# A hybrid attention, convolution and mixture-of-experts layer on one core: the second norm's scale and shift moved to the experts' transposed rows, f32 router logits, another PSUM bank for the last projection, first low parts later

## The chip, the cores and the metric

The kernel runs on one core of a Trainium2 chip. The metric is the device time of one execution in microseconds (us). The engines are called by their names in the profile: PE (TensorE matmul), DVE (VectorE), ACT (ScalarE), POOL (GpSimd) and SP (SyncE, which issues the weight loads).

## The reference, cut to what matters

All tensors are f32; there are 1024 tokens of width 1024, and 16 experts with hidden width 1024.

```python
h2 = modulate(rmsnorm(x, g_ffn), sh2, sc2)     # r*g_ffn*(1+sc2) + sh2, per column
aff = softmax(h2 @ w_router)                   # 1024 x 16
g, idx = top_k(aff.T, 128)                     # each expert takes its 128 best tokens
xs = h2[idx]                                   # per expert 128 x 1024
a, u = xs @ w_gate[e], xs @ w_up[e]
y = (silu(a) * u) @ w_down[e] * g
x = x + gt2 * scatter_add(y, idx)
out = rmsnorm(x, g_final)
```

Ahead of this stand the modulation vectors, the first norm, windowed attention woven with a short convolution, and the output projection `x + gt1 * (mix @ w_out)`.

## The kernel before, in words

**f32 from two parts.** The large products keep f32 accuracy by splitting each operand: a high part (a cast) and a low part (the operand minus its high part). Each product is then three matmuls: high by high, high by the weights' low part, the activations' low part by the weights' high part. A matrix of 1024 x 1024 is taken in eight row blocks k; each k takes six matmuls of 128x512, in this order: two high by high, two on the weights' low part, two on the activations' low part. One matrix so takes 48 matmuls. For each k ACT makes the weights' high part (tile `whl`, L1142) and DVE the low part (L1145), from raw f32 rows that SP loads (`split_rows`, `pump`).

**The projection stage.** `project(t)` (L862) projects one tile of 128 tokens, `residual` adds it to x, `rms` squares it on ACT and takes the reciprocal root on POOL (`rstd`), and `gained` (L885) multiplies x by a row S2 that holds g_ffn*(1+sc2). For the last tile (t = 7) the second half of the columns is done in two quarters c = 0, 1, whose PSUM banks are `po2` (L909): a bank of the P0 tag and the bank C1 (`p1(1)`). C1 is also where the sort keeps `pa`, the transposed affinities (L1047).

**Routing.** Beside the projection of tile t, PE, DVE and ACT route tile t-1 (`route`): `turn_x2` transposes x, splits it into high and low parts (`x2s`: ACT L955, DVE L956), `logits_T` multiplies them by the split router weights (`plT` L970, `lgT` L973, `pl` L977), and `finish_h2` (L930) makes h2 = (x*S2)*rstd + B2 on DVE and has SP store it. Tile 7 goes another way: f32 transposes, and `logits` on f32 operands (L964). Then follow the softmax (L992 is its first step), a sort of each expert's column (MAX8 and MATCH_REPLACE8, L1057 and L1059) and merges of sorted lists (L1020, L1021, L1077). The smallest kept affinity of each expert is `thr` (L1225).

**The step to the experts.** From `thr`: a mask, the places of the chosen tokens (`place`, `choose`: `pos`, `oh`, `pi`, `idx`), and `gather(e)`, an indirect DMA on POOL that fetches the 128 rows of h2 (tile `xr`). The first weights, the gate matrix of expert 0, are split ahead of this, in the tail of the projection stage (`pre_split` L1192).

**An expert.** `turn_x(e)` (L1310) calls `transpose_split`: eight transposes on PE into two PSUM tiles (`xTp`, four blocks of 128x128 each), two casts on ACT and two subtractions on DVE, all reading PSUM. `gate_part` is the 48 matmuls `pg`, `up_part` the 48 `pu`, `down_part` the 48 `py`; ACT takes the Silu of `pg` (tile `hid`), DVE multiplies it by `pu` (L1335), `turn_h` transposes and splits the result (`hTt`).

**What sets the order.** PE's order is the written one: `turn_x(e+2)` is called from the `up_part` of expert e+1 after three quarters of its matmuls, then come the last 12 `pu`, and then the `pg` of expert e+2, which are the first to use the transposed rows. ACT's and DVE's order in the expert stage is set by a list scheduler at build time; each engine then runs its instructions strictly in that order.

Of the kernel before, what the change touches and what calls it, by code (L numbers as in the profile page):

```python
# [9 lines left out]
F32 = mybir.dt.float32  # L10
# [75 lines left out]
def tile_layer(ctx, tc, x, c, cx, c_ctx, w_ada, b_ada, g_mix, w_in, conv_w, sink, w_out, g_ffn,  # L86
# [562 lines left out]
    def router_consts():  # L649
# [28 lines left out]
        rt.update(triu=triu, iota1=iota1, tokid=tokid, wr=wr, lbias=lbias)  # L678
# [148 lines left out]
    rowsb, s_rows1 = crow["a"], crow["sa"]  # L827
    rowsc, s_rows2 = slots.get((2, D), F32, "rowsB")
    GT1, S2, B2 = rowsb[:, 0], rowsb[:, 1], rowsc[:, 0]
    bcast_row(B2, rows_d[1])  # L830
    bcast_row(S2, rows_d[2])
    gf = wm("gf")
    bcast_row(gf, g_ffn[0])
    nc.vector.scalar_tensor_tensor(S2, S2, 1.0, gf, op0=OP.add, op1=OP.mult)

    triu, iota1, tokid, wr, lbias = [rt[k] for k in ('triu', 'iota1', 'tokid', 'wr', 'lbias')]

    wmem = work.tile([128, 384], F32R, tag="mp", name="wrs")
    wrs, ident2 = shaped(wmem, (KC, 2, NE)), wmem[:32, 256:272].bitcast(F32)
    nc.vector.tensor_copy(wrs[:, :, 0], wr)  # L840
    nc.vector.tensor_tensor(wrs[:, :, 1], wr, wrs[:, :, 0].bitcast(F32), op=OP.subtract)
    nc.vector.tensor_tensor(wmem[:32, 256:272], ident[:32, 0:16], ident[:32, 16:32], op=OP.add)

    fold, sign = wmem[:, 272:336].bitcast(F32), wmem[:, 336:337].bitcast(F32)
    nc.vector.tensor_tensor(wmem[:, 272:336], ident[:, 0:64], ident[:, 64:128], op=OP.add)
# [16 lines left out]
    def project(t):  # L862
# [22 lines left out]
        def gained(cols):  # L885

            nc.vector.tensor_tensor(h2_of[t][:, cols], xt[:, cols], S2[:, cols], op=OP.mult)

        if t < NT - 1:
# [7 lines left out]
            gained(slice(0, D))  # L897
        else:
# [9 lines left out]
            gained(slice(0, 512))  # L908
            po2 = [p2(0, "po")[:, 0], p1(1, "po")]  # L909
            for c in range(2):  # L910
                cols = slice(512 + 256 * c, 768 + 256 * c)
                for k in range(KC):
                    hi, lo = ah[:, 0, k], ah[:, 1, k]
                    for a, j, first, last in ((hi, 0, k == 0, False), (hi, 1, False, False), (lo, 0, False, k == KC - 1)):
                        mm(po2[c][:, 0:256], a, wo[k // 4, 1][j][:, k % 4, 256 * c:256 * c + 256],
                           start=first, stop=last, skip_group_check=True)
                        yield 0.108
                with tc.high_priority():
                    nc.vector.tensor_tensor(xt[:, cols], po2[c][:, 0:256], xt[:, cols], op=OP.add)
                    nc.scalar.activation(h2_of[t][:, cols], xt[:, cols], AF.Square, accum_out=ssq[:, 8 + c:9 + c])  # L920
                gained(cols)
# [8 lines left out]
    def finish_h2(t):  # L930
        h2 = h2_of.pop(t)
        x2_of.pop(t)
        nc.vector.scalar_tensor_tensor(h2, h2, rstd[:, t:t + 1], B2, op0=OP.mult, op1=OP.add)
        h2_done[t] = h2
        if t < NT - 2:
            store_h2(t)
# [6 lines left out]
    def turn_x2(t, g, ks=None):  # L943
        if t < NT - 1:
            x2T_of[t, g] = (wm, w4)[g]("x2s", (4, 2, 128), F32R)
        elif g == 0:
            x2T_of[t] = wm("x2T")
# [18 lines left out]
    def logits_T(t):  # L966

        pl = p1(0, "plT")
        for k in range(KC):
            mm(pl[:2 * NE, :256], wrs[:, k].rearrange("p a b -> p (a b)"),  # L970
               x2T_of[t, k // 4][:, k % 4].rearrange("p a b -> p (a b)"), start=k == 0, stop=k == KC - 1)
        lgT = work.tile([32, 256], F32, tag="up", name="lgT")
        nc.scalar.copy(lgT, pl[:32, :256])  # L973
        yield 0.8
        pl_of[t] = p1(0, "pl")
        for i in range(2):
            mm(pl_of[t][:, :NE], lgT[:, i * 128:(i + 1) * 128], ident2, start=i == 0, stop=i == 1)  # L977
# [220 lines left out]
    with order_of:  # L1198
# [5 lines left out]
        slots.put(*wo[0, 1][2:], *wo[1, 1][2:], s_rows1)  # L1204
# [7 lines left out]
        slots.put(s_rows2)  # L1212
# [5 lines left out]
        pre_split((2,))  # L1218
        split_rows("g", 0, 3, (0,))
# [91 lines left out]
    def turn_x(e):  # L1311
        st[e] = {"x": transpose_split(xrow.pop(e), "xT")}
# [195 lines left out]
```

## Time and profile before

| | |
|---|---|
| median of 3 runs | 1176.4 us (1175.99 to 1176.52) |
| the profiled execution | 1177.61 us, its span 1175.8 us |
| mean granted TensorE clock | 0.96 of full speed |
| PE busy | 1064.8 us (91%) |
| DVE busy | 982.2 us (84%) |
| ACT busy | 770.2 us (66%) |
| POOL busy | 357.1 us (30%) |

All times in rows are microseconds from the start of the span; the profiled execution took 1.8 us more than its span. The stages by time: to 440 everything ahead of the output projection, 440 to 545 the projection of tiles 0 to 7 with the routing of the tile before, 545 to 592 the last quarter matmuls, the rest of sorting and the step to the experts, 592 to 1127 the experts, then the end. A share of busy time alone does not tell what bounds a stage: that is read from the waits and the chain of work that ended last.

### The profile page before, as it was taken

The page shows a single profiled execution, that of the slowest core. Times are in us where ns is not written, and L with a number is a line of the kernel's source. Part 1 is how long each engine was busy: PE and PEld are TensorE (multiplying, and loading weights), DVE is VectorE, ACT ScalarE, POOL GpSimd, SP SyncE. Part 2 cuts the span into 40 slices and gives each one's busy share as a digit, 9 for nine tenths or more (in the row PEclk, how much of TensorE's full clock was granted, in tenths as well). Part 3 has the DMA queues.
Part 4 walks back from the last instruction along what each step waited for, and adds up shares of the span by engine and source line. Part 5 has one row for each costly group of instructions (what it writes and reads, how often), then busy time and mean ns, then how long its engine had stood idle before and what let it go on. Part 6 is the DMA issues. An engine that isn't in the chain of part 4 may idle for free.

```text
span 1175.8 us, 15607 instructions
## 1 busy us (share of the span) xinstructions
PE 1064.8 (91%) x5462; PEld 873.8 (74%) x5462; DVE 982.2 (84%) x1673; ACT 770.2 (66%) x1066; POOL 357.1 (30%) x301
## 2 busy tenths in 40 slices
PE   5786889999899998997399999999999999999992
PEld 1675666888788877776288888888888888888871
DVE  6887446887878786599789999999999999999985
ACT  6666545766666743232177888778788788888863
POOL 0457662211303141221204333223333323331015
PEclk9898989999999999999599999999999999999996
DMA  9644540100101175437579999999999999999555
GB/s 375 225 162 143 164 141 19 37 19 1 54 1 37 32 286 201 154 118 266 214 277 370 394 389 389 390 387 391 407 390 388 391 391 387 408 392 389 211 199 213
DMA packets 89496, 288.17 MB, mean 245 GB/s; under 512 B 6901, under 2 KB 20673, under 8 KB 88394
## 3 DMA queue, kind: packets, MB, share of 16 engines
q1 hardware_dynamic: 84666, 269.88, 60.3%
q0 software_dynamic: 4752, 17.30, 5.5%
q8 instruction: 43, 0.70, 0.2%
q14 instruction: 35, 0.29, 0.1%
HBM read 266.17 MB, written 20.99 MB: 244 GB/s over the span
## 4 chain that ended last, share of the span: by engine, by line
PE 74%; DVE 12%; issue 6%; ACT 4%; DMA 2%; POOL 1%; POOLq 0%; ACTq 0%; DVEq 0%
PE pg L1297 15%; PE pu L1297 15%; PE py L1297 14%; PE po L878 5%; PE ps_cv L731 3%; PE ps_cv L730 3%; PE ps_cv L732 3%; PE pt L622 2%; PE po_att L613 2%; PE ps_s L565 1%; PE xTp L1283 1%; PE hTtp L1283 1%; PE ps_s L563 1%; PE pq L520 1%; PE ps_q L501 1%
## 5 line engine op out<-in xcount | busy, mean ns | idle before, releaser
L1145 DVE TENSOR_TENSOR whl<-raw,whl 128x1024 fp32r<-128x1024 f32 x384 | 456.4, 1225 | 30.7 <-ACT whl L1142 19.2
L1142 ACT CAST whl<-raw 128x1024 fp32r<-128x1024 f32 x384 | 401.2, 1054 | 104.0 <-PE pu L1297 37.3
L1297 PE MATMUL pg<-whl,xT 128*128 128x512 f32 x768 | 186.5, 396 | 0.0
L1297 PE MATMUL pu<-whl,xT 128*128 128x512 f32 x768 | 180.9, 391 | 0.0
L1297 PE MATMUL py<-whl,hTt 128*128 128x512 f32 x768 | 176.8, 389 | 0.2 <-ACT hTt L1285 0.2
L1297 PEld LDWEIGHTS py<-whl,hTt 128*128 128x128 f32 x768 | 144.1, 188 | 30.4 <-ACT hTt L1285 0.5
L1297 PEld LDWEIGHTS pu<-whl,xT 128*128 128x128 f32 x768 | 143.0, 188 | 30.0 <-issue 0.8
L1297 PEld LDWEIGHTS pg<-whl,xT 128*128 128x128 f32 x768 | 143.0, 189 | 29.3 <-ACT xT L1285 0.2
L1262 POOL TENSOR_SCALAR oh<-iota,pos 128x128 bf16<-128x128 f32 x108 | 103.8, 976 | 9.6 <-DVE pos L1247 9.1
L1355 POOL DMA_INDIRECT acc_d<-yt,idx x15 | 35.1, 2342 | 197.9 <-DVE yt L1343 197.9
L730 PE MATMUL ps_cv<-hTh,wcs 128*128 128x512 f32 x192 | 80.8, 421 | 0.0
L1307 POOL DMA_INDIRECT xr<-h_d,idx x16 | 21.8, 1360 | 189.8 <-DVE gate_w L1273 189.8
L463 POOL TENSOR_TENSOR acc<-acc,wmod 128x1024 f32<-128x1024 f32 x28 | 69.2, 2491 | 30.1 <-ACT wmod L461 29.5
L625 ACT CAST pth<-pt 128x512 fp32r<-128x512 f32 (+1 forms) x88 | 46.2, 525 | 46.1 <-PE pt L622 45.9
L732 PE MATMUL ps_cv<-hTh,wcs 128*128 128x512 f32 x192 | 75.6, 394 | 0.0
L731 PE MATMUL ps_cv<-hTl,wcs 128*128 128x512 f32 x192 | 75.5, 393 | 0.0
L626 DVE TENSOR_TENSOR pth<-pt,pth 128x512 fp32r<-128x512 f32 (+1 forms) x88 | 53.9, 614 | 20.4 <-ACT pth L625 19.4
L878 PE MATMUL po<-woh,ah 128*128 128x512 f32 x240 | 69.0, 401 | 0.5 <-ACT woh L223 0.5
L711 POOL TENSOR_TENSOR wcs<-wcr,wcs 128x1024 fp32r<-128x1024 f32 x12 | 28.6, 2388 | 109.6 <-ACT wcs L710 87.0
L575 DVE CUSTOM_DVE_ANT_0 sm<-ps_s,maskt,sink 128x640 f32<-128x640 f32 (+1 forms) x56 | 48.3, 863 | 6.8 <-PE ps_s L565 6.3
L578 ACT ACTIVATE sm<-sm,negm 128x640 f32<-128x640 f32 (+1 forms) x64 | 51.6, 807 | 2.8 <-DVE negm L577 2.7
L878 PEld LDWEIGHTS po<-woh,ah 128*128 128x128 f32 x240 | 44.4, 191 | 9.6 <-ACT woh L223 0.9
(293 smaller groups left out, 1837.2 us busy)
## 6 DMA issues: line engine op xcount, KB each, us to landing
raw<-in_w_gate_dram SPq DMA_DIRECT2D x64, 1024.0 KB, 9.2
raw<-in_w_up_dram SPq DMA_DIRECT2D x64, 1024.0 KB, 7.9
raw<-in_w_down_dram SPq DMA_DIRECT2D x64, 1024.0 KB, 9.5
wmod<-in_w_ada_dram SPq DMA_DIRECT2D x32, 512.0 KB, 3.8
wa<-in_w_ada_dram SPq DMA_DIRECT2D x8, 1024.0 KB, 5.1
wcr<-in_w_in_dram SPq DMA_DIRECT2D x12, 512.0 KB, 3.8
xt<-in_x_dram SPq DMA_DIRECT2D x4, 1024.0 KB, 20.6
wor<-in_w_out_dram SPq DMA_DIRECT2D x4, 1024.0 KB
```

Source lines behind the costliest of these rows:

```text
L463: nc.gpsimd.tensor_tensor(acc, acc, wt, op=OP.add)
L575: nc.vector.tensor_tensor_reduce(dst, src, mk, op0=OP.add, op1=OP.max, scale=1.0, scalar=sink8[:, h:h + 1], accum_out=mx[:, b, h:h + 1])
L578: nc.scalar.activation(sm, sm, AF.Exp, bias=negm[:, b, h:h + 1], scale=0.125, accum_out=esum[:, b, h:h + 1])
L626: nc.vector.tensor_tensor(pth[:, 1, :n], pt[:, :n], pth[:, 0, :n].bitcast(F32), op=OP.subtract)
L730: mm(ps, wsp[:, 0, k], hi, start=k == 0, stop=False)
L731: mm(ps, wsp[:, 0, k], lo, start=False, stop=False)
L732: mm(ps, wsp[:, 1, k], hi, start=False, stop=k == KC - 1)
L878: mm(po[n], a, wo[k // 4, n][j][:, k % 4], start=first, stop=last)
L1142: nc.scalar.copy(w[:, 0], t[:, k % 2])
L1145: low = nc.vector.tensor_tensor(w[:, 1], t[:, k % 2], w[:, 0].bitcast(F32), op=OP.subtract)
L1262: nc.gpsimd.tensor_scalar(oh[:, t], iota1, pos[:, t, 0, e:e + 1], None, op0=OP.is_equal)
L1297: mm(ps[n], a_hl[:, a, k], w[:, j, n * 512:(n + 1) * 512], start=first, stop=last)
```

## The change

1. `gained`, S2, B2 and their rows are gone. `finish_h2` becomes one ACT activation h2 = x*rstd. Two memory slots of `rowsA`/`rowsB` go back to the pool of slots earlier, or are never taken, so that weight loads are issued into them earlier.
2. The scale and shift come in `turn_x(e)`, on the transposed rows, where they are one value per partition (`s2T`, `b2T`, 128x1 per block of 128 columns). For e < 2 eight ACT activations (128x128) write the high parts from PSUM and eight DVE `tensor_scalar` write the f32 rows. For e >= 2 eight ACT activations write the f32 rows back over `xr`, then two ACT casts make the high parts from there. The two low parts on DVE now read `xr`.
3. All tiles' router logits are f32 products as tile 7's were; the split, `logits_T`, `lgT` go.
4. The last tile's quarters use the bank of `po[1]` and a P0 bank; C1 is left to the sort.
5. The low parts of the first gate matrix (k = 0 to 3) move from the projection's tail to behind the choice of tokens for expert 1 (k = 0, 1) and behind `place(slice(2, NE))` (k = 2, 3).

```diff
@@ project @@
-        def gained(cols):
-            nc.vector.tensor_tensor(h2_of[t][:, cols], xt[:, cols], S2[:, cols], op=OP.mult)
...
-            po2 = [p2(0, "po")[:, 0], p1(1, "po")]
+            po2 = [po[1], p2(0, "po")[:, 0]]
@@ finish_h2 @@
-        x2_of.pop(t)
-        nc.vector.scalar_tensor_tensor(h2, h2, rstd[:, t:t + 1], B2, op0=OP.mult, op1=OP.add)
+        nc.scalar.activation(h2, x2_of.pop(t), AF.Copy, scale=rstd[:, t:t + 1])
@@ turn_x2 @@
-        if t < NT - 1:
-            hi, lo = [x2T_of[t, g][:, :, i] for i in range(2)]
-            ph = ph.rearrange("p (a b) -> p a b", a=4)
-            nc.scalar.copy(hi, ph)
-            nc.vector.tensor_tensor(lo, ph, hi.bitcast(F32), op=OP.subtract)
-        else:
-            nc.scalar.copy(x2T_of[t][:, ks[0] * 128:(ks[-1] + 1) * 128], ph)
+        nc.scalar.copy(x2T_of[t][:, ks[0] * 128:(ks[-1] + 1) * 128], ph)
@@ route @@
-            yield 1.3
-            yield from logits_T(t)
+            yield 1.6
+            logits(t, range(0, 4))
+            yield 0.9
+            logits(t, range(4, 8))
@@ pre_split, the tail @@
-            split_rows("g", 0, k)
+            split_rows("g", 0, k, (0,))
...
-        pre_split((2,))
-        split_rows("g", 0, 3, (0,))
+        pre_split((2, 3))
@@ turn_x @@
-        st[e] = {"x": transpose_split(xrow.pop(e), "xT")}
+        for g in range(2):
+            cols = slice(512 * g, 512 * g + 512)
+            ps = p1(g, "xTp")
...
+            for k in range(4):
+                c = slice(k * 128, (k + 1) * 128)
+                row = xr[:, cols][:, c]
+                sc2, sh2 = s2T[:, 4 * g + k:4 * g + k + 1], b2T[:, 4 * g + k:4 * g + k + 1]
+                if e < 2:
+                    nc.scalar.activation(hi[:, c], ps[:, c], AF.Identity, scale=sc2, bias=sh2)
+                    nc.vector.tensor_scalar(row, ps[:, c], sc2, sh2, op0=OP.mult, op1=OP.add)
+                else:
+                    nc.scalar.activation(row, ps[:, c], AF.Identity, scale=sc2, bias=sh2)
+            if e >= 2:
+                nc.scalar.copy(hi, xr[:, cols])
+            nc.vector.tensor_tensor(lo, xr[:, cols], hi.bitcast(F32), op=OP.subtract)
@@ the step to the experts @@
-    after(split_rows("g", 0, 3, (1,)), chosen)
+    for k in (0, 1):
+        after(split_rows("g", 0, k, (1,)), chosen)
     idx1 = choose(1)
     gather(1)
     place(slice(2, NE))
+    for k in (2, 3):
+        after(split_rows("g", 0, k, (1,)), chosen)
```

The order of the built programs changes with it. Three places matter.

First DVE, around the end of `up_part`, here for expert 2's rows (`whl` is a low part of weights, `xT` a low part of the transposed rows, `hid` the product with `pu`). Before:

```order
1065 L1145 TENSOR_TENSOR whl_5925<-raw_5569,whl_5925 128x1024
1066 L1145 TENSOR_TENSOR whl_5934<-raw_5569,whl_5934 128x1024
1067 L1286 TENSOR_TENSOR xT_5888<-xTp,xT_5888 128x512 x2
1068 L1145 TENSOR_TENSOR whl_5967<-raw_5589,whl_5967 128x1024
1069 L1335 TENSOR_TENSOR hid<-hid,pu 128x1024
1070 L1145 TENSOR_TENSOR whl_5976<-raw_5589,whl_5976 128x1024
```

With the change:

```order
1036 L1106 TENSOR_TENSOR whl_5885<-raw_5521,whl_5885 128x1024
1037 L1106 TENSOR_TENSOR whl_5894<-raw_5521,whl_5894 128x1024
1038 L1316 TENSOR_TENSOR hid<-hid,pu 128x1024
1039 L1106 TENSOR_TENSOR whl_5927<-raw_5541,whl_5927 128x1024
1040 L1292 TENSOR_TENSOR xT_5840<-xr,xT_5840 128x512
1041 L1106 TENSOR_TENSOR whl_5936<-raw_5541,whl_5936 128x1024
1042 L1292 TENSOR_TENSOR xT_5840<-xr,xT_5840 128x512
```

Both `xT` stood ahead of one `whl` and of `hid`; now the first stands behind `hid` and that `whl`, and the second behind one more `whl`. It is so for experts 2 to 15.

Second ACT at the same place, with the change (before, the two casts `xT<-xTp` stood where the x8 row stands, and nothing else lay between the weights' casts):

```order
503 L1103 CAST whl_5885<-raw_5521 128x1024
504 L1103 CAST whl_5894<-raw_5521 128x1024
505 L1289 ACTIVATE xr<-xTp,b2T,s2T 128x128 x8
506 L1103 CAST whl_5927<-raw_5541 128x1024
507 L1291 CAST xT_5840<-xr 128x512
508 L1103 CAST whl_5936<-raw_5541 128x1024
509 L1291 CAST xT_5840<-xr 128x512
```

All eight scalings stand ahead of the cast of `whl_5927`, whose low part is DVE's row behind `hid`; the two casts of the rows stand behind that.

Third PE, at the end of the first of the last tile's two quarters (`po` are its matmuls, L915 and now L897; `pa` the sort's transposes of the tile before; `pl` logits). Before:

```order
1833 L915 MATMUL po<-wol_4066,ah_5052 128x256
1834 L1048 MATMUL pa<-wrs,affh 64x64
1835 L915 MATMUL po<-woh_4065,ah_5052 128x256
1836 L964 MATMUL pl<-wr,x2T 128x16 x4
1837 L915 MATMUL po<-woh_4065,ah_5052 128x256
1838 L915 MATMUL po<-wol_4066,ah_5052 128x256
1839 L915 MATMUL po<-woh_4065,ah_5052 128x256
1840 L915 MATMUL po<-woh_4011,ah_5052 128x256
```

With the change:

```order
1834 L897 MATMUL po<-woh_4065,ah_4992 128x256
1835 L936 MATMUL pl<-wr,x2T 128x16 x4
1836 L897 MATMUL po<-woh_4065,ah_4992 128x256
1837 L897 MATMUL po<-wol_4066,ah_4992 128x256
1838 L897 MATMUL po<-woh_4065,ah_4992 128x256
1839 L1009 MATMUL pa<-wmem,affh 64x64
1840 L897 MATMUL po<-woh_4011,ah_4992 128x256
```

`pa` moved from inside the first quarter to its end, just ahead of the second quarter's first matmul (`woh_4011`), with which it no longer shares a bank.

## Rows read from the trace of the kernel before

**Rows 1.** Stretches: start:end, length, busy us (count) by engine, PEclk, DMA share, GB/s.

```profile
545.00:592.00 47.00, 19.41 (x123) 16.80 (x122) 39.68 (x194) 9.65 (x21) 10.55 (x18) 0.62 0.63 229
592.00:1127.00 535.00, 534.28 (x2561) 441.36 (x2560) 504.63 (x501) 429.22 (x445) 152.41 (x132) 1.00 0.97 368
```

**Rows 2.** Chain that ended last, 660 to 700, right behind eight transposes: start, length, what.

```profile
681.79 2.76 PE pu L1297 x12
684.56 2.72 PE pg L1297 x12
```

**Rows 3.** Waits of the expert stage, 592 to 1127: total, times, longest.

```profile
ACT whl L1142 <- PE pg L1297: 34.8, 104, 2.2
```

**Rows 4.** Timeline of ACT, 679 to 696; in brackets the idle time before.

```profile
681.91 1.07 ACT L1285 CAST xT<-xTp 128x512 fp32r<-128x512 f32 x2
683.22 1.05 ACT L1142 CAST whl<-raw 128x1024 fp32r<-128x1024 f32 x1 [0.24 <-PE pu L1297]
```

**Rows 5.** Timeline of DVE, 679 to 696: start, length, instruction.

```profile
683.18 1.28 DVE L1286 TENSOR_TENSOR xT<-xTp,xT 128x512 fp32r<-128x512 f32 x2
684.38 1.22 DVE L1145 TENSOR_TENSOR whl<-raw,whl 128x1024 fp32r<-128x1024 f32 x1
685.51 1.21 DVE L1335 TENSOR_TENSOR hid<-hid,pu 128x1024 f32<-128x1024 f32 x1
```

**Rows 6.** Timeline of PE, 545 to 592.

```profile
548.53 0.96 PE L964 MATMUL pl<-wr,x2T 128*128 128x16 f32 x8
...
556.78 0.58 PE L915 MATMUL po<-woh,ah 128*128 128x256 f32 x1 [6.83 <-DVE sa L1050]
```

**Rows 7.** Timeline of DVE, 545 to 592.

```profile
563.38 0.42 DVE L919 TENSOR_TENSOR xres<-po,xres 128x256 f32<-128x256 f32 x1 [0.56 <-PE po L915]
...
565.59 0.23 DVE L992 SCALAR_TENSOR_TENSOR aff<-pl,rstd,lbias 128x16 f32<-128x16 f32 x1
565.74 1.27 DVE L933 SCALAR_TENSOR_TENSOR h<-h,rstd,rowsB 128x1024 f32<-128x1024 f32 x1
566.93 0.21 DVE L1020 TENSOR_TENSOR sa<-ss 32x64 f32<-32x64 f32 x1
...
570.53 1.20 DVE L1145 TENSOR_TENSOR whl<-raw,whl 128x1024 fp32r<-128x1024 f32 x1
...
578.81 0.28 DVE L1225 TENSOR_REDUCE thr<-L 16x1 f32<-16x128 f32 x1
```

**Rows 8.** Groups of PE by form: busy, mean ns of one, idle before.

```profile
L970 PE MATMUL plT<-x2s,wrs 128*32 128x256 f32 x56 | 8.4, 283 | 1.5 <-DVE x2s L956 1.3
L977 PE MATMUL pl<-wrs,lgT 32*128 32x16 f32 x28 | 4.3, 263 | 0.0
```

**Rows 9.** Timeline of DVE, 588 to 600, the start of expert 0.

```profile
590.54 0.69 DVE L1286 TENSOR_TENSOR xT<-xTp,xT 128x512 fp32r<-128x512 f32 x1 [0.58 <-ACT xT L1285]
```

**Rows 10.** Group of DVE by form: busy, mean ns of one.

```profile
L294 DVE TENSOR_SCALAR hf<-ps_xt,mscale,mshift 128x256 f32<-128x256 f32 x4 | 2.1, 538 | 0.7 <-PE ps_xt L286 0.7
```

**Rows 11.** Groups of ACT by form: busy, mean ns of one.

```profile
L1285 ACT CAST xT<-xTp 128x512 fp32r<-128x512 f32 x32 | 17.2, 587 | 17.6 <-PE xTp L1283 17.6
...
L290 ACT ACTIVATE hf<-ps_xt,mshift,mscale 128x512 f32<-128x512 f32 x4 | 3.1, 773 | 0.0
...
L290 ACT ACTIVATE hf<-ps_xt,mshift,mscale 128x256 f32<-128x256 f32 x4 | 2.2, 560 | 4.6 <-DVE mscale L261 4.6
...
L296 ACT CAST hTh<-hfs 128x512 fp32r<-128x512 f32 x4 | 2.4, 610 | 5.8 <-DVE hfs L294 5.8
```

**Rows 12.** Timeline of PE at two earlier pauses.

```profile
84.37 0.39 PE L318 MATMUL ps_kv<-wkvh,hTl 128*128 128x256 f32 x1 [2.25 <-DVE hTl L292]
...
181.56 0.51 PE L563 MATMUL ps_s<-kcv,qT 128*128 128x256 f32 x2 [1.95 <-DVE bias L489]
```

**Rows 13.** Stretches behind these pauses, columns as in rows 1.

```profile
85.10:88.50 3.40, 3.40 (x17) 3.35 (x17) 2.52 (x3) 3.40 (x5) 0.00 (x0) 0.50 0.37 134
...
182.00:185.40 3.40, 3.40 (x20) 2.91 (x19) 0.91 (x3) 2.00 (x3) 0.00 (x0) 1.00 0.08 19
```

More of the change, by code (lines that the diff above doesn't have):

```diff
@@ L677, in router_consts @@
         yield
-        rt.update(triu=triu, iota1=iota1, tokid=tokid, wr=wr, lbias=lbias)
+        rt.update(triu=triu, iota1=iota1, tokid=tokid, wr=wr, lbias=lbias, s2T=s2T, b2T=b2T)
     def attention():
@@ L826, in tile_layer @@
     wo_split(3)
[L827 to L845, printed above, removed]
+    slots.put(crow["sa"])
+    triu, iota1, tokid, wr, lbias, s2T, b2T = [rt[k] for k in ('triu', 'iota1', 'tokid', 'wr', 'lbias', 's2T', 'b2T')]
+    wmem = work.tile([128, 384], F32, tag="mp", name="wmem")
+    fold, sign = wmem[:, 0:64], wmem[:, 64:65]
+    nc.vector.tensor_tensor(fold, ident[:, 0:64], ident[:, 64:128], op=OP.add)
     for i in range(4):
@@ L896, in project @@
                 rms(xt, t, h2_of[t])
-            gained(slice(0, D))
         else:
@@ L907, in project @@
                 nc.scalar.activation(h2_of[t][:, 0:512], xt[:, 0:512], AF.Square, accum_out=ssq[:, t:t + 1])
-            gained(slice(0, 512))
-            po2 = [p2(0, "po")[:, 0], p1(1, "po")]
+            po2 = [po[1], p2(0, "po")[:, 0]]
             for c in range(2):
@@ L920, in project @@
                     nc.scalar.activation(h2_of[t][:, cols], xt[:, cols], AF.Square, accum_out=ssq[:, 8 + c:9 + c])
-                gained(cols)
             slots.put(s_ah)
@@ L943, in turn_x2 @@
     def turn_x2(t, g, ks=None):
-        if t < NT - 1:
-            x2T_of[t, g] = (wm, w4)[g]("x2s", (4, 2, 128), F32R)
-        elif g == 0:
+        if g == 0:
             x2T_of[t] = wm("x2T")
@@ L951, in turn_x2 @@
             nc.tensor.transpose(ph[:, i * 128:(i + 1) * 128], x2_of[t][:, k * 128:(k + 1) * 128], ident)
-        if t < NT - 1:
-            hi, lo = [x2T_of[t, g][:, :, i] for i in range(2)]
-            ph = ph.rearrange("p (a b) -> p a b", a=4)
-            nc.scalar.copy(hi, ph)
-            nc.vector.tensor_tensor(lo, ph, hi.bitcast(F32), op=OP.subtract)
-        else:
-            nc.scalar.copy(x2T_of[t][:, ks[0] * 128:(ks[-1] + 1) * 128], ph)
+        nc.scalar.copy(x2T_of[t][:, ks[0] * 128:(ks[-1] + 1) * 128], ph)
     def logits(t, ks):
@@ L964, in logits @@
             mm(pl_of[t][:, :NE], x2T_of[t][:, k * 128:(k + 1) * 128], wr[:, k, :], start=k == 0, stop=k == KC - 1)
[L966 to L977, printed above, removed]
     def route(t):
@@ L1203, in tile_layer @@
                         [3.2, once(pre_split, (0,))], [8.0, once(keep_values, NT - 2)], [8.5, once(pre_split, (1,))]])
-        slots.put(*wo[0, 1][2:], *wo[1, 1][2:], s_rows1)
+        slots.put(*wo[0, 1][2:], *wo[1, 1][2:])
         wpairs += [slots.free_list.pop(0) for _ in range(4 - nsp)]
@@ L1211, in tile_layer @@
         finish_h2(NT - 1)
-        slots.put(s_rows2)
         xslots.append(slots.free_list.pop(0))
@@ L1311, in turn_x @@
     def turn_x(e):
-        st[e] = {"x": transpose_split(xrow.pop(e), "xT")}
+        xr = xrow.pop(e)
+        s = xslots.pop(0)
+        dst, _ = slots.get((2, 8, 128), F32R, "xT", slot=s)
+        for g in range(2):
+            cols = slice(512 * g, 512 * g + 512)
+            ps = p1(g, "xTp")
+            for k in range(4):
+                nc.tensor.transpose(ps[:, k * 128:(k + 1) * 128], xr[:, (4 * g + k) * 128:(4 * g + k + 1) * 128], ident)
+            hi, lo = [dst[:, a, 4 * g:4 * g + 4].rearrange("p a b -> p (a b)") for a in range(2)]
+            for k in range(4):
+                c = slice(k * 128, (k + 1) * 128)
[9 more added lines that the diff above has]
+            nc.vector.tensor_tensor(lo, xr[:, cols], hi.bitcast(F32), op=OP.subtract)
+        st[e] = {"x": (dst, s)}
     def turn_h(e):
```

## Prediction

> **What bounds the kernel now.** I read the stretches by stage first, then the chain that ended last, the waits, the timelines of the engines at the places where the change cuts, and last the prices of similar instructions. In the stretches the reader is to see two different limits. From 592 to 1127 PE is busy 534.28 us of 535 at full clock, with DVE at 504.63; from 545 to 592 PE is busy 19.41 of 47 at a mean clock of 0.62, and DVE 39.68 [rows 1]. So the experts are bound by PE without a break: whatever makes PE wait there is paid in full. The step ahead of them is a chain of small things, most of it on DVE.
>
> The chain of the expert stage says the same: eight transposes, twelve `pu` in 2.76 us, then at 684.56 `pg` of the next expert with no gap [rows 2]. I call this moment T. A matmul takes 2.72 / 12 = 0.2267 us. The waits have ACT's casts waiting for PE to give back weight tiles, 34.8 us in 104 waits [rows 3]; none of theirs is for a load, so the weight transfers (DMA share 0.97 [rows 1]) do arrive in time.
>
> Why there is no gap at T now: ACT casts both halves of `xT` right behind the transposes, 681.91 to 682.98 [rows 4], and DVE has both low parts by 684.46, just before T, ahead of one `whl` and of `hid` [rows 5].
>
> In the step, the reader is to see PE's pause of 6.83 us ahead of 556.78, ended by the sort's `sa` [rows 6]: the second quarter of the last tile wants the bank C1, in which `pa` waits to be read. Then tile 7's softmax starts at 565.59 and `thr` at 578.81 [rows 7].
>
> **The change, part by part.**
>
> *The step gets shorter.* With its own bank the second quarter follows the first, so 6.83 us go. Its stretch from 556.78 to the residual at 563.38, 6.6 us, ran at half clock for the most part because of that pause; at full clock I give it 3.9. The softmax then starts at 565.59 - 6.83 - 2.7 = 556.1. From there to `thr` it is now 13.2 us on DVE. In that stretch lie `finish_h2`, 1.19 us up to the next start (565.74 to 566.93), and one low part of 1.20, 1.13 back to back [rows 7]; both go. But the softmax now comes while more of the sort of the tile before is still open: by the listing some ten more merge rows stand behind it, at 0.21 each [rows 7] or 2.1. So 13.2 - 1.2 - 1.1 + 2.1 = 13.0, `thr` at 569.1, a gain of 9.7. Bounds: 7 (the pause alone) and 12 (no merge row added).
>
> *f32 logits.* Off go 8.4 + 4.3 us of records in seven tiles, 1.81 a tile [rows 8]. Tile 7's eight records (four blocks, two passes each) took 0.96 [rows 6]; sixteen are 1.92. So +0.1 a tile; with the overlap of neighbouring records unknown, 0 to 0.3. I count 0.1 in all seven on PE, 0.7, of which waits for the removed DVE split, 1.3 [rows 8], give more than that back: nothing. The DVE work of `gained` and of the split is not on the path that sets the end of the projection; it costs and gives nothing else. `finish_h2` and the f32 copies are on an ACT that is busy 9.65 of 47 us there [rows 1]. Slots that come free earlier let SP issue loads earlier, past nothing that waits for them: nothing.
>
> *Expert 0.* Four low parts, back to back at 1.13 (684.38 to 685.51 [rows 5]), now stand ahead of the last `oh` on DVE, where one stood; DVE had pauses there, so I let `oh`, which now ends 0.58 ahead of 590.54 [rows 9], end 1.2 later (without any pause 3 x 1.13 = 3.4). Behind it come seven scalings of 128 columns ahead of the first low part. The nearest row is 538 ns for 256 columns [rows 10], so between 0.27 and 0.54; I take 0.32, 2.2 in all. The first low part then ends at about 594.1, against 591.23 now [rows 9]. Part of these 2.9 us is cover (four matmuls stand ahead of the first that needs it), but PE starts at half clock here and rises later if it stops. I take +2.5, bounds 1 and 4.
>
> *Experts 2 to 15: the main term.* Times from T. The transposes end at -2.77. ACT scales with two per-partition operands: 773 ns for 512 columns, 560 for 256 [rows 11], so 560 - 213/2 = 0.45 for 128, and neighbours overlap by 0.10 (two casts of `xT` in 1.07 [rows 4], one alone 0.587 [rows 11]), so 0.355 each. Eight end at +0.19. The weight cast (1.05, less the overlap 0.95 [rows 4]) ends at about +1.2, the first cast of the rows (610 ns from SBUF [rows 11]) at +1.74. DVE has no more to do before `hid`, and `hid` needs the last `pu`: it ends at 0.05 + 1.13 = +1.18. The `whl` behind it needs the weight cast: 1.30 to 2.43. Then the first low part of the rows, 0.64 (half of 1.28 [rows 5]) and the signal: +3.16. PE wants the high parts at 0, has them at 1.79, then issues four matmuls, and wants the low part for the fifth, which without any wait is at 4 x 0.2267 = 0.907. It starts at 3.16: **2.25 us lost per expert**, 14 x 2.25 = 31.5. Nothing takes it back: PE has no idle time in the stage to fill. Lower bound: scalings so cheap that only DVE's order counts, 0.05 + 1.13 + 1.13 + 0.64 - 0.907 = 2.05, or 28.7. Upper: no overlap of the scalings, 8 x 0.45, weight cast at 1.9, low part at 3.9: 3.0, or 42.
>
> Here the Trainium skill can be weighed against the rows. Its page "ScalarE: Activation LUTs", section "What ACT_TABLE_LOAD costs", has an activation with immediates at 186 ns + 0.833 ns a column, each per-partition pointer 93 ns more, and neighbours overlapping by 93 ns. By it 128 columns with two pointers take 0.386 back to back, eight end 0.25 later, the loss is 2.5 us and the sum 3.5 us higher. By the rows I keep 2.25.
>
> *Expert 1.* Its first low part stands behind `hid` and two `whl`: 0.05 + 3 x 1.13 + 0.64 = +4.1, PE loses 3.2 in one piece. After a pause of 2.25 the clock was at half for 3.40 us, after one of 1.95 it stayed full [rows 12, 13]. So here I add a fall of the clock, half of 3.40, or 1.7: +4.9, bounds 3.2 and 5.
>
> *The sum.* -9.7 + 2.5 + 4.9 + 31.5 = +29.2. The profiled execution took 1177.6, so 1206.8; the median of the runs is 1.2 lower, so I give **1205.6**.
>
> **The rivals.**
>
> *A, slower still: the clock falls at most experts.* The loss is a pause of 1.79, four matmuls, and one of 0.46, together 2.25; a pause of 2.25 was followed by half clock, one of 1.95 was not [rows 12, 13]. If each of the 14 brings 3.40 us at half clock, it costs 1.7 more each, 24: 1229. Against it: the longest piece is under the 1.95 that left the clock alone, and PE is busy for 30 us before it.
>
> *B, the step is not shorter.* DVE works through the merges at 84% of that stretch (39.68 of 47 [rows 1]); if the sort of the tile before, and not the bank, sets `thr`, only the removed 2.3 us go, and the time is 1213. Against it: DVE's work there can start without the second quarter.
>
> *C, the other side: faster.* The transfers could be what truly sets the expert stage: DMA share 0.97 [rows 1]. Loads are issued as tiles come free, so a pause of PE would leave the queue its work, and PE would make up its 2.25 us out of earlier stock. Then the stage stays at 535 if the stalls fit beside it, and what is left is -9.7 + 2.5, or 1169. It decides if an expert's transfers take as long as PE's work and the 2.25 us together. For it only that share; against it, no cast waits for a load [rows 3], and PE's chain has no gap to be refilled [rows 2]. The skill's page "Perfetto Trace Analysis", section "Roofline", puts the ceiling of one core's 16 DMA engines at about 435 GB/s; the stage moves 368 [rows 1], under it, so by that rule too the transfers have room.
>
> That the change does not do what it says is no rival for the order: an engine runs its listing in order, and the listing shows `xT` behind `hid`.
>
> **How the numbers follow.** My case 0.62 (its own bounds: -12 + 1 + 3.2 + 28.7 = +21, 1197; -7 + 4 + 5 + 42 = +44, 1220), A 0.18 in full or in part, B 0.07, C 0.08, and 0.05 for other mixtures, of which 0.03 end near no change. The range of 1196 to 1230 takes in my case, B and A, and leaves C and the mixtures out. Faster by over 0.2% (2.4 us, about what a measurement of this kernel can tell from no change) 0.09, within 0.03, slower 0.88.
>
> **What would show it.** Right: in the waits of the expert stage `pg` waiting for ACT's `xT` about 1.8 us and for DVE's `xT` about 0.5, fourteen times; each expert 2.25 us longer than now in the chain; `thr` near 569; no `po` wait for `sa`. A would show as half clock right behind those pauses, B as `thr` after 575, C as waits of ACT's casts for loads. A `pg` that starts right behind `pu` in experts 2 to 15 would prove the main term wrong.

## The result and the profile after

The changed kernel takes 1217.62 us, the median of four runs (1214.02 to 1218.43), against 1176.46 (1175.99 to 1177.12) for the kernel before, in four runs as well: the ratio is 1.0337, with a 95% interval of 1.0323 to 1.0352, so +41 us. The forecast was 1205.6 with a range of 1196 to 1230: the right side and the right main cause, with 12 us missing.

The spans of the two profiled executions, 1175.8 and 1216.6, split at five events that both have. The expected values are the terms of the prediction's sum.

| piece | before | after | change | expected |
|---|---|---|---|---|
| to the projection's first matmul | 435.7 | 437.3 | +1.6 | 0 |
| from there to `thr` | 143.1 | 131.5 | -11.7 | -9.7 |
| `thr` to the first `pu` (step, expert 0's gate) | 25.0 | 30.5 | +5.5 | +2.5 |
| first `pu` to first `py` (expert 0's up, expert 1's gate) | 23.1 | 28.9 | +5.8 | +4.9 |
| first `py` to the end | 548.9 | 588.4 | +39.5 | +31.5 |

The first piece is no effect of the change: over the profiled executions of this study that matmul starts at 433.0 to 438.0, in kernels that do the same up to there.

The waits of the changed kernel from 592 to 1160 (total, times, longest) show where PE, which had no wait there before, now stops.

```profile
PE pg L1256 <- ACT xT L1291: 24.6, 14, 1.8
DVE hid L1316 <- PE pu L1256: 18.6, 14, 1.3
PE pg L1256 <- DVE xT L1292: 4.6, 5, 4.0
```

Fourteen pauses of 1.75 us, one for each of experts 2 to 15, wait for the high part of the transposed rows; before each of them DVE stands 1.3 us idle in front of `hid`. One of them, from PE's timeline (start, length, instruction, idle time before):

```profile
797.30 3.01 PE L1256 MATMUL pu<-whl,xT 128*128 128x512 f32 x12
802.05 1.20 PE L1256 MATMUL pg<-whl,xT 128*128 128x512 f32 x4 [1.75 <-ACT xT L1291]
803.40 2.09 PE L1256 MATMUL pg<-whl,xT 128*128 128x512 f32 x8 [0.15 <-DVE xT L1292]
```

ACT's timeline at the same place answers to [rows 4]:

```profile
797.66 2.89 ACT L1289 ACTIVATE xr<-xTp,b2T,s2T 128x128 f32<-128x128 f32 x8
800.41 1.07 ACT L1103 CAST whl<-raw 128x1024 fp32r<-128x1024 f32 x1
801.34 0.66 ACT L1291 CAST xT<-xr 128x512 fp32r<-128x512 f32 x1
```

and DVE's to [rows 5]:

```profile
800.34 1.22 DVE L1316 TENSOR_TENSOR hid<-hid,pu 128x1024 f32<-128x1024 f32 x1 [1.33 <-PE pu L1256]
801.51 1.23 DVE L1106 TENSOR_TENSOR whl<-raw,whl 128x1024 fp32r<-128x1024 f32 x1
802.66 0.69 DVE L1292 TENSOR_TENSOR xT<-xr,xT 128x512 fp32r<-128x512 f32 x1
```

The last `pu` ends at 800.31, the moment T of the prediction. The eight scalings fill ACT until T + 0.24, the weight's cast follows, and only then the cast of the rows; on DVE the rows' low part waits out `hid` and one weight part and ends at T + 3.04. `pg` starts 1.90 late against the start that it had before, and its fifth matmul loses 0.44 more. From one `py` to the next it is 37.3 us, where it was 34.8.

At two of the fourteen pauses the distance is 38.8. The stretches behind one of these two and behind another pause of equal length (columns as in [rows 1], the last but two is the clock) show why:

```profile
839.30:844.40 5.10, 4.96 (x21) 3.38 (x21) 4.26 (x5) 2.50 (x4) 0.00 (x0) 0.67 1.03 420
802.05:805.50 3.45, 3.29 (x19) 2.27 (x19) 3.27 (x5) 2.48 (x3) 0.00 (x0) 1.00 1.02 414
```

Behind the one, part of the time is at half clock (a mean of 0.67 between the levels), and the same twelve `pg` take 5.02 us and not 3.44; behind the other the clock stays full. The two falls begin at 840.7 and 1066.0. A third stretch at half clock, from 1168.4, lies in the last expert's up projection, where PE waits for no `xT`; it makes that projection longer, here in the changed kernel and then in the kernel before:

```profile
1166.99 12.82 PE L1256 MATMUL pu<-whl,xT 128*128 128x512 f32 x48
```

```profile
1127.77 11.18 PE L1297 MATMUL pu<-whl,xT 128*128 128x512 f32 x48
```

### The profile page after: what moved, and what is told of

It reads as the page before. It is cut to its first block, busy times and chain, and to the rows that moved or that the text cites. A ratio compares the mean times of both kernels' runs of the same rounds, so it can differ in the third digit from the quotient of the medians.

```text
span 1216.6 us, 15813 instructions
## 1 busy us (share of the span) xinstructions
PE 1079.2 (89%) x5490; PEld 879.6 (72%) x5490; DVE 970.5 (80%) x1653; ACT 816.2 (67%) x1191; POOL 358.0 (29%) x301
## 4 chain that ended last, share of the span: by engine, by line
PE 64%; DVE 15%; ACT 9%; issue 8%; DMA 3%; POOL 2%; POOLq 0%; ACTq 0%; DVEq 0%; SPq 0%
PE pg L1256 14%; PE py L1256 14%; PE pu L1256 7%; PE po L866 6%; DVE whl L1106 3%; ACT xr L1289 3%; PE ps_cv L731 3%; PE ps_cv L730 3%; PE ps_cv L732 3%; PE pt L622 2%; PE po_att L613 2%; ACT whl L1103 2%; PE ps_s L565 1%; PE hTtp L1242 1%; PE ps_s L563 1%
## 5 line engine op out<-in xcount | busy, mean ns | idle before, releaser
L1256 PE MATMUL pg<-whl,xT 128*128 128x512 f32 x768 | 198.7, 410 | 33.1 <-ACT xT L1291 24.6
L1256 PEld LDWEIGHTS pg<-whl,xT 128*128 128x128 f32 x768 | 144.4, 194 | 74.6 <-ACT xT L1291 30.5
L1256 PEld LDWEIGHTS pu<-whl,xT 128*128 128x128 f32 x768 | 144.1, 189 | 30.5 <-issue 0.8
L1221 POOL TENSOR_SCALAR oh<-iota,pos 128x128 bf16<-128x128 f32 x108 | 116.7, 1093 | 11.8 <-DVE pos L1206 11.2
```

Source lines behind the costliest of these rows:

```text
L1221: nc.gpsimd.tensor_scalar(oh[:, t], iota1, pos[:, t, 0, e:e + 1], None, op0=OP.is_equal)
L1256: mm(ps[n], a_hl[:, a, k], w[:, j, n * 512:(n + 1) * 512], start=first, stop=last)
```

## The experiments

Two theories stood at the start. The first is the prediction's: experts 2 to 15 lose because the scaled rows are late around the end of `up_part`, and the step before them gains because the last projection got its own bank. The rival: the added work itself (2.9 us of scaling on ACT per expert) makes the weight parts late wherever it stands, and the sort on DVE sets `thr` whatever the bank is. Each ratio below is to runs of the kernel before beside the experiment, with medians of 1177.16 to 1178.85 us.

### e1_early: the transposes one quarter earlier

```diff
-        run(up_part(e + 1), (2,), (lambda: turn_x(e + 2),))
+        run(up_part(e + 1), (1,), (lambda: turn_x(e + 2),))
```

> The changed kernel with the transposes of the next expert's rows called one quarter of the up projection (12 matmuls, 2.7 us) earlier; nothing else differs. Theory (the loss in experts 2 to 15 is only lateness of the scaled rows behind the last up matmul: 14 x 2.47 us, plus a fall of the clock of 1.5 us at some of them): the first part for DVE is ready before hid, no wait of pg for xT in these experts, period back to 34.8, time 1178 to 1183. Rival (ACT has 2.9 us more work per expert and DVE reads other operands, so weights come late wherever the transposes stand): the waits move to the weight tiles and more than half of the loss stays, 1200 or more.

Measured: 1194.06 us (1193.21 to 1195.06), 1.0135 of before (1.0120 to 1.0151). Neither number came true: more than half of the loss is gone, not all; an expert takes 36.0 us, where the kernel before has 34.8. PE's wait for `xT` is gone in experts 2 to 15. Its place was taken by a smaller one, in the waits of this run:

```profile
PE pg L1256 <- DVE whl L1106: 11.0, 14, 1.2
```

So both theories hold a part: the lateness is real, and behind it stands a shortage of weight parts.

### e7_early2: two quarters earlier

```diff
-        run(up_part(e + 1), (2,), (lambda: turn_x(e + 2),))
+        run(up_part(e + 1), (0,), (lambda: turn_x(e + 2),))
```

> The changed kernel with the transposes two quarters of the up projection (24 matmuls, 5.4 us) earlier, one more than in e1_early, which kept 1.2 us of wait per expert, for DVE's low parts of the weights. The listing now has both low parts of the rows and two of the weights ahead of hid on DVE. Theory (the loss is DVE's and ACT's lateness around the end of the up projection): no wait of pg in experts 2 to 15, period 34.8, 1177 to 1182, with expert 1's loss still there. Rival (the added work makes DVE's weight parts late wherever it stands): 1190 or more.

Measured: 1188.31 us, 1.0079 (1.0065 to 1.0094); 35.5 us an expert. Neither number came true: no pause of PE in experts 2 to 15 is longer than 0.4 us, but 0.7 us per expert remain. PE's weight loads (PEld) wait for the weights' low parts:

```profile
PEld pg L1256 <- DVE whl L1106: 6.7, 14, 0.6
PEld pu L1256 <- DVE whl L1106: 6.5, 12, 0.8
```

The chain that ended last shows where that comes from (start, length, what):

```profile
679.11 1.55 ACT xr L1289 x5
...
682.01 0.94 ACT whl L1103
...
687.59 1.20 DVE whl L1106
...
689.86 1.23 DVE whl L1106
691.09 0.04 issue
691.13 5.29 PE pg L1256 x22
```

PE waits for a weight's low part, and following that back the chain comes to ACT's scalings. While ACT scales it casts no weights, and the parts that PE has in stock run out some microseconds later.

### e3_noscale: no scale and shift at all

```diff
-        xr = xrow.pop(e)
...
+        st[e] = {"x": transpose_split(xrow.pop(e), "xT")}
```

> The changed kernel with the scale and shift left out altogether: the experts' rows are only transposed and split as in the kernel before, so the experts see x*rstd. Theory (all of the loss in the experts comes from the scaling in turn_x): period 34.8, no wait of pg; what is left is the shorter step less the slower GpSimd one-hots, 1176.4 - 10 + 1.8 = 1168, up to 1170. Rival (f32 logits, the later low parts or the earlier loads cost too): 1172 or more.

Measured: 1168.61 us, 0.9927 (0.9912 to 0.9942). 34.8 us an expert, no wait of `pg`. The whole loss in the experts is the scaling's, and the rest of the change is worth 8.5 us. (Without the scale and shift the experts see other rows than the reference's; this kernel only prices the parts.)

### e2_bank: the banks alone

```diff
-            po2 = [p2(0, "po")[:, 0], p1(1, "po")]
+            po2 = [po[1], p2(0, "po")[:, 0]]
```

> The kernel before with only the two banks of the last projection's quarters changed (po[1] and P0's bank, C1 left to the sort). Theory (the shared bank held the second quarter and so the threshold): the 6.83 us pause goes, tile 7's softmax near 556.5, thr near 572 as the two removed DVE pieces (2.3 us) are still there, time 1169 to 1170.5. Rival (the sort's order on DVE sets the threshold anyway): 1174 to 1176.5.

Measured: 1176.50 us, 0.9992 (0.9983 to 1.0001). DVE's timeline of this run:

```profile
557.06 0.23 DVE L992 SCALAR_TENSOR_TENSOR aff<-pl,rstd,lbias 128x16 f32<-128x16 f32 x1
...
577.36 0.27 DVE L1225 TENSOR_REDUCE thr<-L 16x1 f32<-16x128 f32 x1
```

The number is the rival's. The pause of 6.83 us is gone and tile 7's softmax starts 8.5 us earlier than in [rows 7], yet `thr` comes only 1.5 earlier: softmax to `thr` has grown from 13.2 to 20.3 us. The stretches before `thr` say why (the third busy time is DVE's), first of the kernel before, then of this one:

```profile
546.00:578.80 32.80, 12.03 (x70) 10.81 (x68) 30.40 (x167) 8.22 (x19) 4.57 (x12) 0.65 0.66 249
```

```profile
546.00:577.40 31.40, 9.96 (x76) 9.03 (x76) 29.59 (x168) 7.97 (x17) 3.22 (x12) 0.70 0.76 275
```

DVE is busy 30.40 of 32.80 us in the kernel before, most of it with sorting and merging, and PE's pause lay beside that. Work that comes to DVE sooner could win no more than the 2.4 us in which it stood idle there.

### e5_oldbank: the change's step with the old banks

On top of e3_noscale:

```diff
-            po2 = [po[1], p2(0, "po")[:, 0]]
+            po2 = [p2(0, "po")[:, 0], p1(1, "po")]
...
```

> The kernel of e3_noscale (the change without scale and shift, 1168.6 us) with the two old banks back for the last projection's quarters. Theory after e2_bank (what held the threshold was DVE's backlog of sorting and merging, which the removed DVE work of the projection stage shortened; the bank matters little by itself): thr within 2 us of where e3_noscale has it, 1168.5 to 1171. Rival (the bank's pause of 6.8 us comes back and is what counted, as the prediction had it): 1174 or more.

Measured: 1167.51 us, 0.9908 (0.9890 to 0.9925), beside 0.9927 for e3_noscale: the banks give nothing that the times could show from this side either. This rests on the times alone.

### e6_logits: the f32 logits alone

```diff
-            hi, lo = [x2T_of[t, g][:, :, i] for i in range(2)]
...
-            nc.vector.tensor_tensor(lo, ph, hi.bitcast(F32), op=OP.subtract)
...
-            yield from logits_T(t)
+            logits(t, range(0, 4))
+            yield 0.9
+            logits(t, range(4, 8))
```

> The kernel before with only the f32 router logits (no split of the transposed tiles: 14 DVE subtractions of 0.675 us and the transposed logits go, 16 f32 matmul passes a tile come). Theory (DVE's backlog): DVE has 9 us less to do ahead of the sorts, thr 2 to 6 us earlier, 1171 to 1175. Rival (that DVE work lies beside PE and is not on the path): 1176 to 1178.

Measured: 1173.97 us, 0.9968 (0.9955 to 0.9980). From the projection's first matmul to `thr` it takes 140.15 us, 3.0 less than before. PE's matmuls had waited 1.3 us in all for the removed split ([rows 8]). The reading that fits with e2_bank is that work on DVE which hardly delays the projection's matmuls is paid at its end, because the sorts queue behind it; no row of this run shows that queue by itself.

### e4_lows: the first low parts back in the tail

```diff
-            split_rows("g", 0, k, (0,))
+            split_rows("g", 0, k)
...
+    after(split_rows("g", 0, 3, (1,)), chosen)
```

> The changed kernel with the first gate matrix's low parts back where the kernel before has them (k = 0 to 2 in the projection's tail, k = 3 behind the choice for expert 1). Theory (four low parts back to back on DVE slow GpSimd's two one-hots beside them from 0.63 to 2.04 us each, and PE's first transposes wait behind their matmuls): one-hots back at about 0.6 us, transposes of expert 0 about 10.0 us behind thr instead of 11.8, thr 0.5 to 2.3 later; time 1215 to 1218, so no difference that this kernel's falls of the clock let one see; the trace decides. Rival (the one-hots are slower for another reason): they stay near 2.0 us.

Measured: 1219.46 us, 1.0356 (1.0340 to 1.0372); as expected the times hardly part it from the change. The trace does. First GpSimd's one-hots for expert 1 beside DVE's four low parts, in the changed kernel, on POOL and on DVE:

```profile
575.49 4.07 POOL L1221 TENSOR_SCALAR oh<-iota,pos 128x128 bf16<-128x128 f32 x2
```

```profile
574.38 4.79 DVE L1106 TENSOR_TENSOR whl<-raw,whl 128x1024 fp32r<-128x1024 f32 x4
```

and the same two one-hots in this run, where a single subtraction ends 0.2 us into them:

```profile
574.60 1.26 POOL L1222 TENSOR_SCALAR oh<-iota,pos 128x128 bf16<-128x128 f32 x2
```

They take 0.6 us each alone and 1.7 and 2.4 beside the subtractions. PE's transposes for expert 0 stand behind their matmuls in PE's order: they start 10.0 us behind `thr` here, 11.8 in the changed kernel. In return `thr` itself comes 3.5 us later here (135.0 us after the projection's first matmul, where the change has 131.5), more than the 0.5 to 2.3 that were expected. The Trainium skill states this in "GPSIMD Engine Reference", section "1. Specifications": GpSimd shares its SBUF interfaces with VectorE and contends with VectorE instructions that have two SBUF inputs, which these subtractions have; the durations agree with it.

### e8_best: experts 0 and 1 scaled on ACT alone, low parts behind expert 1's choice

```diff
-        run(up_part(e + 1), (2,), (lambda: turn_x(e + 2),))
+        run(up_part(e + 1), (0,), (lambda: turn_x(e + 2),))
...
-                if e < 2:
+                if e < 0:
...
+    for k in range(4):
+        after(split_rows("g", 0, k, (1,)), idx1)
     place(slice(2, NE))
```

> e7_early2 with two more edits: experts 0 and 1 are scaled on ACT like the others (no scaling on DVE), and the four first low parts wait for the choice of expert 1 (behind GpSimd's two one-hots, not beside them). Theory: one-hots back at 0.6 us (1.8 us), expert 0's gate stage 2.5 to 3.5 us shorter, expert 1's 4 to 5.9 us shorter: 1167 to 1171, under both kernels. Rival (the four low parts now stand late in front of expert 0's first matmuls): a wait of pg for whl at the start of expert 0, 1172 or more.

Measured: 1182.93 us, 1.0037 (1.0024 to 1.0050). The one-hots are back at 0.6 us. But the four low parts now stand on DVE ahead of `pos`, which holds the bank of the second transposes, as PE's timeline has it:

```profile
580.66 1.12 PE L1279 MATMUL xTp<-ident,xr 128*128 128x128 f32 x4 [2.20 <-DVE pos L1205]
```

and experts 2 to 15 keep the 35.5 us of e7_early2, which the theory had left out: 14 x 0.7 is 10 us of what it missed. The rival's number is nearer, but its sign did not come: no `pg` waits for `whl` at the start of expert 0.

### e9_spread: turn_x in four parts

On top of e8_best, with a `turn_x` that takes the parts it is to do:

```diff
...
-        run(up_part(e + 1), (0,), (lambda: turn_x(e + 2),))
+        run(up_part(e + 1), (0, 1, 2, 3), (lambda: turn_x(e + 2, (0,)), lambda: turn_x(e + 2, (1,)), lambda: turn_x(e + 2, (2,)), lambda: turn_x(e + 2, (3,))))
```

> The kernel of e8_best (1182.9 us) with turn_x cut into four parts of two transposes and two scalings, one behind each quarter of the up projection, so that ACT does at most two scalings (0.7 us) between two casts of weights, not eight (2.9 us). Theory (what is left in e7_early2 and e8_best, 35.5 us an expert where the kernel before has 34.8, is ACT's block of eight scalings, which holds back the weights' casts by more than their lead of about 1 us): period 34.8 to 35.0, time 1172 to 1175. Rival (DVE's order or total work is the limit, the same in both): period stays 35.5, 1181 to 1185.

Measured: 1179.86 us, 1.0016 (1.0007 to 1.0026). The mechanism is right: with the same work on ACT and DVE no wait is left in experts 2 to 15, and an expert takes 34.9 us. The time is not, since the same four parts in experts 0 and 1, all in one place, made PE's transposes wait for ACT to read the PSUM tile that they write, in the waits from 570 to 610:

```profile
PE xTp L1286 <- ACT xr L1289: 5.7, 4, 2.5
```

### e10_pool: scale and shift on GpSimd, on the token rows

On top of e3_noscale, with the rows S2 and B2 made again:

```diff
...
+        nc.gpsimd.tensor_tensor(h2, h2, S2, op=OP.mult)
+        nc.gpsimd.tensor_tensor(h2, h2, B2, op=OP.add)
...
```

> The kernel of e3_noscale (1168.6 us) with scale and shift put back on the token rows, but on GpSimd (two 128x1024 operations per tile behind ACT's x*rstd) and not on DVE nor on the experts' rows; it computes the reference's result. Theory (the front gains because DVE is rid of work ahead of the threshold, the experts lose only by turn_x): GpSimd has the room (20 us busy of 105 in the projection), the stores of h2 end well ahead of the first gather, 1168 to 1172. Rival (the last tile's h2 comes too late for the gather, or GpSimd's work slows DVE's sorts): 1174 or more, with a wait of the first transposes or a later thr.

Measured: 1187.39 us, 1.0077 (1.0062 to 1.0093). The rival's second half is right: `thr` comes 151.1 us after the projection's first matmul, 20 more than in e3_noscale. Two timelines of this run, of POOL and of DVE at the same time, show how (`L` are the sorts' merges):

```profile
517.29 2.37 POOL L922 TENSOR_TENSOR h<-h,rowsA 128x1024 f32<-128x1024 f32 x1 [1.26 <-ACT h L921]
519.74 2.40 POOL L923 TENSOR_TENSOR h<-h,rowsB 128x1024 f32<-128x1024 f32 x1
```

```profile
517.17 0.21 DVE L991 TENSOR_TENSOR L<-L 16x64 f32<-16x64 f32 x1
517.32 2.43 DVE L992 TENSOR_TENSOR L<-L 16x64 f32<-16x64 f32 x1
519.78 2.50 DVE L1048 SCALAR_TENSOR_TENSOR L<-xq,L 16x128 f32<-16x128 f32 x1
```

A merge of 0.21 us that begins just behind a multiplication on GpSimd takes 2.43, as long as that runs, and the next one, behind the addition, 2.50. Here it is GpSimd that holds DVE, on the path that sets `thr`. The Trainium skill's page "SBUF — State Buffer" (section "SBUF: two separate sides") says that of a GpSimd operation and a VectorE operation with two SBUF inputs the one that starts first keeps the shared ports for its whole instruction and the other is blocked; these rows agree with it where GpSimd is first. That GpSimd stands still behind VectorE is not shown: the one-hots of e4_lows only take longer there.

### e11_quarters and e12_halves: the start mended

`turn_x` takes the blocks that it is to do, and all scalings are on ACT:

```diff
...
+    after(split_rows("g", 0, 0, (1,)), chosen)
...
+    placed = place(slice(2, NE))
+    for k in range(1, 4):
+        after(split_rows("g", 0, k, (1,)), placed)
...
+    def parted(e):
+        return [lambda ks=ks: turn_x(e, ks) for ks in ((0, 1), (2, 3), (4, 5), (6, 7))]
...
+    run(up_part(0), (0, 1, 2, 3), parted(1))
...
+        run(up_part(e + 1), (0, 1, 2, 3), parted(e + 2))
```

and for e12_halves on top of it:

```diff
-        return [lambda ks=ks: turn_x(e, ks) for ks in ((0, 1), (2, 3), (4, 5), (6, 7))]
+        return [lambda ks=ks: turn_x(e, ks) for ks in ((0, 1, 2, 3), (4, 5, 6, 7))]
...
-    run(up_part(0), (0, 1, 2, 3), parted(1))
+    run(up_part(0), (1, 2), parted(1))
...
-        run(up_part(e + 1), (0, 1, 2, 3), parted(e + 2))
+        run(up_part(e + 1), (1, 2), parted(e + 2))
```

> The kernel of e9_spread (1179.9 us) with its start mended: expert 0's eight transposes again ahead of its scalings (in quarters they waited for one another, 5.5 us for what took 1.9), expert 1's quarters behind the quarters of expert 0's up projection, and the first low parts in DVE's pauses (k = 0 behind expert 1's one-hots, k = 1 to 3 behind the places of all experts). Theory (e9_spread has no wait left in experts 2 to 15, its loss is all in experts 0 and 1, about 8 us more than e3_noscale): 1171 to 1174, 3 to 6 us under the kernel before. Rival (the scaling of experts 0 and 1 costs as much in any order): 1177 or more.

> e11_quarters with two halves (four transposes and four scalings each, behind the second and the third quarter of the up projection) in place of four quarters. Theory (ACT's longest stretch without a cast of weights decides, here 1.4 us against a lead of about 1, and each extra part costs PE some 0.06 us): within 2 us of e11_quarters, waits of pg or pu for weights of 0.4 us at most. Rival (any block of more than two scalings starves the weights): a period of 35.3 or more, 1176 to 1180.

Measured: e11_quarters 1173.24 us, 0.9953 (0.9940 to 0.9966); e12_halves 1170.66 us, 0.9930 (0.9913 to 0.9947). Both beat both kernels; e12_halves lies 2.6 us under e11_quarters, a little more than the 2 that were expected. PE's busy time in e12_halves from 600 to 1115:

```profile
600.00:1115.00 515.00, 515.00 (x2479) 425.17 (x2478) 490.23 (x487) 447.65 (x550) 217.46 (x132) 1.00 0.99 375
```

No wait is left, and an expert takes 34.8 us with all of the scaling in it. ACT's timeline shows the two blocks of four between the casts of weights:

```profile
635.34 1.50 ACT L1290 ACTIVATE xr<-xTp,b2T,s2T 128x128 f32<-128x128 f32 x4
636.72 1.05 ACT L1103 CAST whl<-raw 128x1024 fp32r<-128x1024 f32 x1
637.66 0.64 ACT L1293 CAST xT<-xr 128x512 fp32r<-128x512 f32 x1
638.18 1.07 ACT L1103 CAST whl<-raw 128x1024 fp32r<-128x1024 f32 x1
639.13 1.52 ACT L1290 ACTIVATE xr<-xTp,b2T,s2T 128x128 f32<-128x128 f32 x4
```

Two blocks of 1.5 us are borne, one of 2.9 is not (e7_early2). The quarters cost PE 0.1 us an expert more, with four changes to transposes and back in place of two.

## Why the prediction was right, point by point

**Experts 2 to 15, right, the term sized 10% low.** The pause sat where the prediction put it, with ACT's eight scalings and DVE's order as its two causes; experiments e3_noscale and e12_halves show that nothing else is in it. The prediction said 2.25 us and 14 x 2.25 = 31.5; measured are 2.5 us and 35. The prices were right: eight scalings took 2.89 us (expected 8 x 0.355 and an overhang of 0.1), the low part ended at T + 3.04 (2.43 + 0.64 = 3.07 expected). What failed is the reference on PE: "without any wait is at 4 x 0.2267 = 0.907" counts from the end of the last `pu`, while in a running chain `pg` starts 0.16 us ahead of that end; and of the 2.5 us only 1.90 and 0.44 are there by the fifth matmul, the rest comes in the matmuls behind it. The rule of the Trainium skill's "ScalarE: Activation LUTs" (section "What ACT_TABLE_LOAD costs"), by which the prediction worked out an estimate of 0.386 us a scaling, would have given 2.5. The trace has 0.36 (2.89 / 8), so the sum by the rule came out nearer by luck.

**The clock, rival A, in part.** The prediction let the clock fall at expert 1 only; in the profiled execution it fell at 2 of the 14 as well, 1.5 us each, +3.0. The half clock in the last expert's up projection adds 1.7, but e3_noscale, without any scaling, has it too: from the first `py` of expert 14 to that of expert 15 it is 29.3 us in both, and 27.7 in the kernel before. So no run ties that 1.7 to the pauses. Rival A's limit ("the longest piece is under the 1.95 that left the clock alone") was no limit: pauses of 1.75 were followed by either level.

**The step before the experts, the size near by luck and the cause wrong.** `thr` came at 568.8, the prediction said 569.1; from the projection's first matmul 11.7 us went, where 9.7 were forecast. But the step "with its own bank the second quarter follows the first, so 6.83 us go" is refuted by e2_bank and e5_oldbank: the banks give `thr` 1.2 us, not 6.8. The gain of 11.7 us comes for the most part from work that DVE no longer has ahead of the sorts: 3.0 from the f32 logits (e6_logits) and 3.5 from the low parts moved out of the tail (e4_lows against the change). With the 1.2 of the banks 4 are left for `gained` and the row form of `finish_h2` together, if the parts add up; these two were not tried by themselves, so that share is argued and not shown. The prediction had named most of this "not on the path" and counted it as nothing. Rival B's condition, that the sort on DVE sets `thr`, was true; its price was wrong, as it left out the DVE work removed upstream. That work is not worth its busy time either: from the projection's first matmul to `thr` DVE is busy 28.7 us less, here before and then with the change:

```profile
435.68:578.81 143.13, 117.52 (x582) 94.57 (x580) 115.50 (x442) 44.07 (x96) 27.18 (x52) 0.91 0.56 203
```

```profile
437.31:568.77 131.46, 114.16 (x610) 96.25 (x608) 86.85 (x407) 49.84 (x97) 15.25 (x52) 0.94 0.58 213
```

**Expert 0, too low.** +5.5 where 2.5 was expected. Counted from `thr`, the rows' first low part ends at 17.9 us, where it ended at 12.4 before. Two terms were too small. DVE's last `oh` ends 2.9 later than before, not 1.2: GpSimd's one-hots, slowed by the low parts beside them (e4_lows), hold up the chain to it, which the prediction did not have. And DVE's seven scalings behind it take 3.2 us, not 2.2, or 2.6 less the 0.58 of idle time that stood there: expected at 0.32 us each, they came in turns with ACT's on the same PSUM tile, as DVE's timeline shows:

```profile
583.68 0.76 DVE L1287 TENSOR_SCALAR xr<-xTp,s2T,b2T 128x128 f32<-128x128 f32 x2 [0.21 <-ACT xT L1286]
584.61 0.76 DVE L1287 TENSOR_SCALAR xr<-xTp,s2T,b2T 128x128 f32<-128x128 f32 x2 [0.18 <-ACT xT L1286]
```

Two scalings here and two on ACT take 0.93 us, 0.47 a scaling. In e3_noscale, with the same slow one-hots and no scaling, `thr` to the first `pu` takes 26.3 us, 1.3 more than before; so 4.2 of the 5.5 come with the scaling.

**Expert 1, near.** +5.8 where 4.9 was expected. Its interleaved scalings on DVE let `hid` start 0.74 us behind T, which the prediction had at 0.05:

```profile
610.53 0.72 DVE L1287 TENSOR_SCALAR xr<-xTp,s2T,b2T 128x128 f32<-128x128 f32 x2
611.17 1.21 DVE L1316 TENSOR_TENSOR hid<-hid,pu 128x1024 f32<-128x1024 f32 x1
```

**Rival C, no.** No cast of weights waits for a load in the expert stage, and PE's pauses were paid in full.

Of the 12 us that were missing the table has 11.5: +1.6 before the projection, -2.0 in the step, +3.0 at expert 0, +0.9 at expert 1, +8.0 behind it (35 instead of 31.5 in the pauses, the clock 3.0 at two of them and 1.7 in the last expert). The first two have nothing to do with each other, and that they nearly cancel is luck too.

## What to carry to other kernels

Where one engine is the bound without a gap, an operation moved to another engine costs by where it stands in that engine's order and by how long it holds up the stream that feeds the bound, not by its busy time: here the same scalings cost 2.5 us an expert in one block behind three quarters, 0.7 in one block earlier, and nothing in two blocks. A long pause on a chart is no proof of what sets the end: before it is counted, look whether another engine is full right beside it, and then look at all work of that engine upstream, also where it delays nothing at the time (here 28.7 us of it less brought `thr` 11.7 forward). Two engines that read the same memory can slow each other; a move that overlaps them anew needs a price for it.

## What the runs showed that was not expected

GpSimd's one-hot of 128x128 takes 0.6 us alone and 1.7 to 2.4 beside DVE's subtractions of two SBUF operands (e4_lows); in the other direction a DVE merge of 0.21 us takes 2.43 beside one multiplication on GpSimd (e10_pool). And TensorE's clock fell to half at 2 of 14 pauses of the same 1.75 us in the same place of the same loop (at 3 of 14 in e4_lows): the pauses and the matmuls ahead of them look the same, and what decides stays open.
